# A short convolution's first products: ten of them in front, units loaded twice, squares summed by DMAs

## The chip, the cores and the metric

The kernel runs on one core of a Trainium2 chip. The metric is the device time of one execution in microseconds (us); the time of a version is the median of its runs. TensorE (PE) multiplies matrices, VectorE (DVE) and ScalarE (ACT) work element by element, GpSimd (POOL) and SyncE (SP) here only start DMAs. Each engine executes its own instructions in order, and semaphores tie the engines together.

## The reference

A decoder trunk of two layers on a sequence of 1024 positions with 1024 features, in float32. Layer 0 mixes by a short gated convolution, layer 1 by dilated attention; each is followed by a SwiGLU block. The change is in layer 0's mixer, and there in its first projection:

```python
def rms_norm(x, g):
    xf = x.astype(jnp.float32)
    y = xf * lax.rsqrt(jnp.mean(xf * xf, axis=-1, keepdims=True) + EPS)
    return (y * g.astype(jnp.float32)).astype(x.dtype)

def short_conv_mixer(h, w_in, conv_k, w_out):
    b, c, u = jnp.split(h @ w_in, 3, axis=-1)
    y = lax.conv_general_dilated(c * u, conv_k[:, None, :], window_strides=(1,),
        padding=[(CONV_WIDTH - 1, 0)], dimension_numbers=("NWC", "WIO", "NWC"),
        feature_group_count=D_MODEL)
    return (b * y) @ w_out

h = rms_norm(x, mix_norm[0])
x = x + short_conv_mixer(h, conv_w_in[0], conv_kernel[0], conv_w_out[0])
```

## The kernel before

A float32 product is made of three matmuls in a reduced format: every operand is split into a high part (a copy by ACT, L137, L497 or L803) and a low part (the difference, by DVE, L138, L498 or L804), and L505 to L507 multiply high by high, high by low and low by high.

The projection `h @ w_in` goes by Winograd's form of Strassen's method. The weights are cut into twelve units u of two tiles each (a "raw" tile is 128 x 1024 floats, 512 KB). A unit has seven products m, each of four times three matmuls of 128x128 by 128x512, and so of twelve. Products 1, 2 and 4 take a quarter of the unit's weights as it is; 6, 7, 5 and 3 take sums of quarters, which `add_pair` makes on DVE (L185, "combo") ahead of the split. The other side, operand m, is a quarter of X times the norm's gain or a sum of such quarters; `operands` makes the seven of them once, in the order 1, 2, 6, 7, 5, 4, 3, and all units share them. The scale of the norm (the mean of squares) is applied later, to the products' results, so products can start before it is known.

The results of a unit gather in two or three of the eight banks of PSUM ("p", "q", "r"); `save` copies a bank out (L511, ACT), `add` adds a bank to such a copy (L515, DVE). `first(u)` is the add for products 1 and 2 of a unit, and frees the bank q.

The order of products is written by hand in `unit_order`: before, (0,1), (1,1), (0,2), (1,2), (2,1), (2,2), (3,1), then the sixth and seventh products of units 0 and 1 and so on, a pair (u, m) being product m of unit u. `mix` says beside which product which other work is recorded: `start(n)` runs after the n-th product, `next(prep)` goes one step on in `operands`, `ensure(at(u, m))` makes weights up to (u, m). What is recorded first stands first in each engine's queue. `squares` squares tiles of X on ACT (L394, L398) and adds them into the tile `acc` on DVE (L400); `stats` then sums over partitions by eight small matmuls (L417), and a second step spreads the result (L433).

Weights come by DMAs from SP. `load_first` issues the first ones in a fixed order, halves of X between them; `load_raw(upto)` issues later ones (L151), up to a number that each unit's table `ahead` gives for a product. Tiles live in a ring of 41 pages: a page that is freed is taken again, and who takes it waits for its last reader.

Of the kernel before, what the change touches and what calls it, by code (L numbers as in the profile page):

```python
# [23 lines left out]
HALF = 512  # L24
# [70 lines left out]
def trunk(ctx: ExitStack, tc: tile.TileContext, x, gains_in, cwi, ck, cwo, wqkv, wo, relb,  # L95
# [19 lines left out]
    def half(h):  # L115
        return slice(h * HALF, (h + 1) * HALF)
# [61 lines left out]
    def add_pair(u, rows, w, eng, upto, low=()):  # L178


        t = {}

        def combo(a, b, op):
            c = half_page("combo")[:, :w]
            eng.tensor_tensor(out=c, in0=a, in1=b, op=op)  # L185
# [65 lines left out]
    def unit_order(nu, conv):  # L251

        order = [(0, 1), (1, 1), (0, 2), (1, 2), (2, 1), (2, 2), (3, 1)]
        if conv:
            order += [(0, 6), (1, 6), (3, 2)] + [(u, m) for m in (7, 5, 4, 3) for u in (0, 1)]
            order += [(2, 6), (2, 5), (2, 7)]
        else:
            order += [(3, 2)] + [(u, m) for m in (6, 7, 4, 5, 3) for u in (0, 1)] + [(2, 6), (2, 5), (2, 7)]
        order += [(3, 6), (2, 4), (2, 3), (3, 5), (3, 7), (4, 1)] + [(4, 2)] * conv + [(3, 4), (3, 3)]
# [11 lines left out]
    def add_units(key, nu, column):  # L271
# [1 line left out]
        units, slabs, base = [], {}, len(raw_src)  # L273
        raw_base[key] = base
        for u in range(nu):
            rows = ((0, 1), (2, 5), (3, 6), (4, 7))[u] if u < 4 else (2 * u, 2 * u + 1)
            for n in range(2):
                slabs[rows[n]] = column(u, n)
            if u < 4 or key == CONV:
                a = ((2, 5), (3, 7), (4, 7), (4, 9))[u] if u < 4 else (2 * u + 3, 2 * u + 3)  # L280
                ahead = {m: a[m > 2] for m in WINOGRAD}
                if key != CONV and u < 2:
# [12 lines left out]
        raw_src.extend(slabs[r] for r in range(2 * nu))  # L295
        ops.extend(units[u][m] for u, m in unit_order(nu, key == CONV))

    def add_down(key, w, pairs, chunk, last):
# [174 lines left out]
    class Strassen:  # L473
# [73 lines left out]
        def whole(self, u, m, d):  # L547
# [16 lines left out]
            if m == 2 and u > 3 or (u, m) == (0, 4):  # L564
                for x in (u,) if u else range(4):
                    self.out(x, (0, 0), self.first(x))
                    del self.st[x]["u1"]

# [222 lines left out]
    class Conv(Strassen):  # L791
# [12 lines left out]
            nc.vector.scalar_tensor_tensor(lo, t, self.norm.gain(n), hi, op0=ALU.mult, op1=ALU.subtract)  # L804

        def squares(self, ns, h):
            for n in ns:
                self.norm.square(n, h * HALF, h * HALF + HALF, eng=nc.vector)

        def operands(self):  # L810
            gain, stt = self.norm.gain, nc.vector.scalar_tensor_tensor
# [7 lines left out]
            t3, t2 = [half_page("t3") for k in range(4)], [half_page("t2") for k in range(4)]  # L819
            for k in range(4):  # L820
                nc.scalar.activation(t3[k], X[k][:, b], AF.Identity, scale=gain(k))
            for m in (6, 7, 3):
                combos[CONV, 0](m)
            lo = None
            for k in range(4):
                stt(t3[k], X[4 + k][:, b], gain(4 + k), t3[k], op0=ALU.mult, op1=ALU.subtract)
# [16 lines left out]
            yield  # L843
            for k in range(4):
                self.operand(5, k, k, X[k][:, b])
            for k in range(4):
                stt(t2[k], X[4 + k][:, a], gain(4 + k), t2[k], op0=ALU.mult, op1=ALU.subtract)
            yield
# [3 lines left out]
            yield  # L852
            for k in range(4):
                self.operand(3, k, 4 + k, X[4 + k][:, b])
            X[:4] = [None] * 4

        def pad(self, t, h):

# [101 lines left out]
        def mix(self, group1):  # L960
            norm = self.norm
            prep = self.operands()
            stats = norm.stats(0, S)
            late = [(k, h) for h in range(2) for k in range(4, KT)]

            def start(n):
                if n == 0:
# [2 lines left out]
                elif n == 1:  # L970
                    next(prep)
                elif n == 2:
                    ensure(self.at(3, 1))
                    next(prep)
                elif n == 3:
                    ensure(self.at(0, 6))
                    combos[CONV, 1](6)
                    combos[CONV, 1](7)
                    next(prep)
                    ensure(self.at(1, 6))  # L980
                    self.squares(range(4), 1)
                elif n == 4:
                    ensure(self.at(0, 7))
                    next(prep)
                elif n == 7:
                    ensure(self.at(1, 7))
                    next(prep)
                    ensure(self.at(1, 5))
                elif n == 8:
                    next(prep)  # L990
                    ensure(self.at(1, 4))
                elif n == 11:
                    self.first(1)
                    next(prep, None)
                    ensure(self.at(1, 3))
                elif n == 18:
                    self.ahead = 3
                for _ in range({7: 1, 9: 2, 11: 2, 12: 3}.get(n, 0)):
                    k, h = late.pop(0)
                    self.squares((k,), h)  # L1000
                    if h:
                        X[k] = None

            def gather():
                for u in range(1, 4):
                    if "q" in self.st[u]:
                        self.first(u)
                next(stats)

            def spread():  # L1010
# [788 lines left out]
```

## Time and profile before

| | |
|---|---|
| median of 3 runs | 2215.94 us (2215.3 to 2217.3) |
| the profiled execution | 2215.37 us, of which the profile's span is 2213.6 |
| mean granted PE clock | 0.985 |
| DMA from 4 to 24 us | 300 to 414 GB/s |
| DMA from 26 to 35 us | none |
| last product of this stage, (11,3) | starts at 260.19 us |

A row of the timeline gives the start, the duration, the engine, the line, the operation, out<-in and the shapes; the bracket is the idle time of the engine before it and what ended it. "PE" rows are matmuls, "PEld" the loads of their weights. The matmuls of one product start 0.23 us apart at full clock though each is shown as 0.39 long, because they are pipelined.

### The profile page before, as it was taken

Reading aid. Unit: us, or ns where it says so; the run is one execution under the profiler, and the core shown is the slowest. Engines: PE = TensorE matmul, PEld = TensorE weight load, DVE = VectorE, ACT = ScalarE, POOL = GpSimd, SP = SyncE. Lnnn points to the kernel's source line nnn. Section 1 sums busy time; section 2 is a strip of 40 time slices with the busy share of each in tenths; the row PEclk is TensorE's granted clock in tenths of the full one; section 3 lists DMA queues with packets and bytes.
Section 4 is the critical chain, followed back from the end, with each engine's and each line's share of the span. In section 5 each row is a group of like instructions: output and inputs, shape, how many; then the busy total and the mean of one; then the engine's idle time right before and its main releaser. Section 6 shows DMA issues by size and latency. Waiting matters only on the chain.

```text
span 2213.6 us, 30526 instructions
## 1 busy us (share of the span) xinstructions
PE 2143.2 (97%) x11138; PEld 1829.8 (83%) x11138; DVE 1769.8 (80%) x3255; ACT 998.4 (45%) x1808; POOL 147.9 (7%) x196
## 2 busy tenths in 40 slices
PE   7899999899999999999999999999899999999998
PEld 5788887688888878878999999887678888878887
DVE  7797758888888798965677767868988888889886
ACT  6433425444444444434455555534534444444435
POOL 0000000010101000010111111110010101000000
PEclk9999999999999999999999999999999999999999
DMA  4122541222323374423333333544113323266432
GB/s 154 53 84 74 208 131 51 86 98 90 117 93 114 106 269 153 131 86 131 90 90 91 90 90 83 168 130 140 62 72 102 113 96 119 96 218 210 155 93 77
DMA packets 131263, 255.30 MB, mean 115 GB/s; under 512 B 47386, under 2 KB 58666, under 8 KB 131114
## 3 DMA queue, kind: packets, MB, share of 16 engines
q1 hardware_dynamic: 75978, 184.80, 26.2%
q0 software_dynamic: 13968, 45.46, 5.6%
q10 hardware_dynamic: 41168, 23.10, 3.6%
q8 instruction: 88, 1.44, 0.3%
q14 instruction: 61, 0.50, 0.1%
HBM read 187.04 MB, written 66.26 MB: 114 GB/s over the span
## 4 chain that ended last, share of the span: by engine, by line
PE 79%; DVE 11%; ACT 4%; DMA 3%; issue 2%; ACTq 0%; SPq 0%; DVEq 0%
PE bank L505 16%; PE bank L507 16%; PE bank L506 16%; PE bank L346 5%; PE bank L348 5%; PE bank L347 5%; PE bank L1425 4%; PE bank L600 2%; PE bank L599 2%; PE bank L597 2%; DVE b L498 2%; DVE w L138 2%; PE bank L1353 1%; PE bank L1352 1%; DVE x L438 1%
## 5 line engine op out<-in xcount | busy, mean ns | idle before, releaser
L505 PE MATMUL bank<-b,w 128*128 128x512 f32 x1784 | 706.1, 396 | 27.2 <-DVE part L515 7.3
L507 PE MATMUL bank<-b,w 128*128 128x512 f32 x1784 | 702.7, 394 | 15.8 <-DVE w L138 15.8
L506 PE MATMUL bank<-b,w 128*128 128x512 f32 x1784 | 702.7, 394 | 2.1 <-DVE b L498 2.1
L505 PEld LDWEIGHTS bank<-b,w 128*128 128x128 f32 x1784 | 339.8, 190 | 102.4 <-ACT w L137 10.5
L507 PEld LDWEIGHTS bank<-b,w 128*128 128x128 f32 x1784 | 339.4, 190 | 91.9 <-DVE w L138 20.3
L506 PEld LDWEIGHTS bank<-b,w 128*128 128x128 f32 x1784 | 340.0, 191 | 73.3 <-DVE b L498 2.9
L137 ACT ACTIVATE w<-combo 128x512 fp32r<-128x512 f32 (+2 forms) x464 | 235.0, 535 | 279.2 <-DVE combo L185 273.4
L138 DVE TENSOR_TENSOR w<-combo,w 128x512 fp32r<-128x512 f32 (+2 forms) x464 | 260.6, 575 | 69.2 <-ACT w L137 67.2
L511 ACT ACTIVATE part<-bank 128x512 f32<-128x512 f32 x168 | 99.2, 594 | 276.1 <-PE bank L507 273.6
L138 DVE TENSOR_TENSOR w<-raw,w 128x512 fp32r<-128x512 f32 (+2 forms) x316 | 168.9, 559 | 20.8 <-ACT w L137 19.1
L515 DVE TENSOR_TENSOR part<-part,bank 128x256 f32<-128x256 f32 (+1 forms) x348 | 158.6, 486 | 31.0 <-PE bank L507 15.5
L137 ACT ACTIVATE w<-raw 128x512 fp32r<-128x512 f32 (+2 forms) x316 | 150.2, 520 | 45.7 <-PE bank L507 11.3
L726 DVE TENSOR_TENSOR x<-x,bank 128x512 f32<-128x512 f32 x168 | 114.2, 680 | 30.9 <-PE bank L507 30.9
L346 PE MATMUL bank<-w_hi,w 128*128 128x512 f32 (+1 forms) x320 | 122.0, 381 | 0.0
L348 PE MATMUL bank<-w_hi,w 128*128 128x512 f32 (+1 forms) x320 | 120.0, 375 | 0.7 <-DVE w L138 0.7
L347 PE MATMUL bank<-w_lo,w 128*128 128x512 f32 (+1 forms) x320 | 119.8, 374 | 0.0
L438 DVE TENSOR_TENSOR x<-x,bank 128x512 f32<-128x512 f32 (+1 forms) x104 | 65.9, 641 | 62.6 <-PE bank L348 53.8
L185 DVE TENSOR_TENSOR combo<-raw 128x512 f32<-128x512 f32 (+1 forms) x160 | 102.9, 643 | 4.3 <-DMA raw<-in_conv_w_in 4.3
L346 PE MATMUL bank<-h_hi,w_hi 128*128 128x512 f32 x256 | 104.6, 409 | 0.7 <-ACT w_hi L137 0.7
L348 PE MATMUL bank<-h_hi,w_lo 128*128 128x512 f32 x256 | 100.2, 391 | 0.7 <-DVE w_lo L138 0.7
L347 PE MATMUL bank<-h_lo,w_hi 128*128 128x512 f32 x256 | 99.9, 390 | 0.0
L1111 ACT ACTIVATE part<-part 128x512 f32<-128x512 f32 x66 | 39.7, 628 | 110.6 <-DVE part L515 110.6
(237 smaller groups left out, 3835.2 us busy)
## 6 DMA issues: line engine op xcount, KB each, us to landing
hin<-part SPq DMA_DIRECT2D x126, 256.0 KB
raw<-in_ffn_w_gate SPq DMA_DIRECT2D x44, 512.0 KB
raw<-in_ffn_w_up SPq DMA_DIRECT2D x44, 512.0 KB
part<-sum POOLq DMA_DIRECT2D x72, 256.0 KB, 3.0
raw<-in_ffn_w_down SPq DMA_DIRECT2D x48, 384.0 KB
x<-spill SPq DMA_DIRECT2D x24, 512.0 KB
raw<-in_attn_w_qkv SPq DMA_DIRECT2D x24, 512.0 KB
raw<-in_conv_w_in SPq DMA_DIRECT2D x21, 512.0 KB
```

Source lines behind the costliest of these rows:

```text
L137: nc.scalar.activation(hi, src, AF.Copy)
L138: eng.tensor_tensor(out=lo, in0=src, in1=hi, op=ALU.subtract)
L185: eng.tensor_tensor(out=c, in0=a, in1=b, op=op)
L346: nc.tensor.matmul(b, whi[:, a], ahi[:, s], start=first, stop=False)
L347: nc.tensor.matmul(b, whi[:, a], alo[:, s], start=False, stop=False)
L348: nc.tensor.matmul(b, wlo[:, a], ahi[:, s], start=False, stop=last)
L505: nc.tensor.matmul(b, hi[:, a], bhi, start=start and k == 0, stop=False, skip_group_check=True)
L506: nc.tensor.matmul(b, hi[:, a], blo, start=False, stop=False, skip_group_check=True)
L507: nc.tensor.matmul(b, lo[:, a], bhi, start=False, stop=k == n - 1, skip_group_check=True)
L511: nc.scalar.activation(t, b, AF.Copy)
L515: nc.vector.tensor_tensor(out=t, in0=t, in1=b, op=ALU.add)
L726: nc.vector.tensor_tensor(out=X[n][:, half(h)], in0=X[n][:, half(h)], in1=b, op=ALU.add)
```

## The change

- **The order of products.** Ten products that need only operands 1 and 2 now stand in front, two of each of units 0 to 4: (3,2), (4,1) and (4,2) come ahead of (0,6). Then come 6, 7, 5 and 4 of units 0 and 1 in turn, (2,6), (2,7), (0,3), (1,3), (2,5), and from (3,6) on the order is as it was, without (4,1) and (4,2). The statistics' two steps hang on (0,3) and (2,5) where they hung on (2,6) and (2,7).
- **Raw tiles.** The table of rows gives the place of each unit's tiles in the order of loads. Units 2, 3 and 4 now have their first tile early, for products 1 and 2, and load it a second time beside their second tile, for the products with m > 2, so that its page is free in between: three loads more. `load_first` issues seven raw tiles where it issued five (tiles 4, 1, 5, 6).
- **Squares.** ACT still squares; the sums into `acc` are now fourteen accumulating DMAs of 256 KB, issued by POOL from page `sq`, for k = 1 to 7 in two halves.
- **Hooks.** `start`, `gather` and `operands` are written anew to go with it: no weight combination stands ahead of operand 6, `first(0)` to `first(4)` are called at fixed places, and all of X is given up after operand 3.

```diff
         def raw(m, n, h):
             load_raw(upto(m))
-            return raw_tile[rows[n]][:, h * w:h * w + w]
+            return raw_tile[rows[2 if n == 0 and m > 2 and len(rows) > 2 else n]][:, h * w:h * w + w]
...
         if conv:
-            order += [(0, 6), (1, 6), (3, 2)] + [(u, m) for m in (7, 5, 4, 3) for u in (0, 1)]
-            order += [(2, 6), (2, 5), (2, 7)]
+            order += [(3, 2), (4, 1), (4, 2)] + [(u, m) for m in (6, 7, 5, 4) for u in (0, 1)]
+            order += [(2, 6), (2, 7), (0, 3), (1, 3), (2, 5)]
...
+            if key == CONV:
+                rows = ((0, 1), (2, 6), (3, 7, 8), (4, 9, 10), (5, 11, 12))[u] if u < 5 else (2 * u + 3, 2 * u + 4)
...
+            for n in range(len(rows)):
+                slabs[rows[n]] = column(u, n % 2)
+            if key == CONV:
+                a = {0: (6, 6, 6, 7, 7), 1: (6, 6, 7, 8, 8), 2: (8, 9, 9, 10, 10), 3: (10, 11, 12, 12, 13),
+                     4: (12, 14, 13, 14, 15)}.get(u, (2 * u + 6,) * 5)
+                ahead = dict(zip((6, 7, 5, 4, 3), a))
+                ahead.update({m: 6 if u < 5 else 2 * u + 6 for m in (1, 2)})
...
         def squares(self, ns, h):
+            norm = self.norm
+            if norm.acc is None:
+                norm.acc, norm.rstd = page("acc"), page("rstd")
             for n in ns:
-                self.norm.square(n, h * HALF, h * HALF + HALF, eng=nc.vector)
+                if n == 0:
+                    nc.scalar.activation(norm.acc[:, half(h)], X[n][:, half(h)], AF.Square)
+                else:
+                    sq = page("sq")[:, :HALF]
+                    nc.scalar.activation(sq, X[n][:, half(h)], AF.Square)
+                    nc.gpsimd.dma_start(out=norm.acc[:, half(h)], in_=sq, accum_op=ALU.add)
...
-            for m in (6, 7, 3):
-                combos[CONV, 0](m)
...
                 elif n == 2:
-                    ensure(self.at(3, 1))
+                    ensure(self.at(4, 1))
+                    self.squares(range(4, KT), 0)
                     next(prep)
                 elif n == 3:
-                    ensure(self.at(0, 6))
-                    combos[CONV, 1](6)
-                    combos[CONV, 1](7)
+                    ensure(self.at(4, 2))
+                    self.first(0)
                     next(prep)
-                    ensure(self.at(1, 6))
                     self.squares(range(4), 1)
                 elif n == 4:
+                    self.first(1)
+                    ensure(self.at(1, 6))
+                elif n == 5:
                     ensure(self.at(0, 7))
+                    self.squares(range(4, KT), 1)
...
-            self.run(start, {(2, 6): gather, (2, 7): spread})
+            self.run(start, {(0, 3): gather, (2, 5): spread})
...
-        for i in range(5):
+        for i in range(7):
             raw_tile[i] = page("raw")
-        raw_state[0] = 5
+        raw_state[0] = 7
...
-        nc.sync.dma_start(raw_tile[4], raw_src[4])
-        nc.sync.dma_start(raw_tile[1], raw_src[1])
+        for i in (4, 1, 5, 6):
+            nc.sync.dma_start(raw_tile[i], raw_src[i])
```

DVE's queue behind the splits for the first six products, before. The combos are those of unit 0's weights, L826 and L827 make operand 6, L498 and L138 are second halves of operands and weights.

```order
L138 TENSOR_TENSOR w<-raw,w 128x512 x3
L185 TENSOR_TENSOR combo<-raw 128x512
L185 TENSOR_TENSOR combo<-combo,raw 128x512
L185 TENSOR_TENSOR combo<-raw 128x512
L185 TENSOR_TENSOR combo<-raw,combo 128x512
L826 SCALAR_TENSOR_TENSOR t_316<-x,gains,t_316 128x512
L827 SCALAR_TENSOR_TENSOR t_320<-x,gains,t_316 128x512
L826 SCALAR_TENSOR_TENSOR t_317<-x,gains,t_317 128x512
L827 SCALAR_TENSOR_TENSOR t_321<-x,gains,t_317 128x512
L498 TENSOR_TENSOR b<-t_320,b 128x512
L138 TENSOR_TENSOR w<-raw,w 128x512
```

The same place in the changed kernel, from the third tile of operand 6 on (L842 to L843 make operand 6, L507 and L138 are second halves, L524 is `add`). Before these rows stand the first half of operand 6 and the three splits for (3,1), (3,2) and (4,1).

```order
L138 TENSOR_TENSOR w<-raw,w 128x512 x3
L842 SCALAR_TENSOR_TENSOR t_323<-x,gains,t_323 128x512
L843 SCALAR_TENSOR_TENSOR t_327<-x,gains,t_323 128x512
L507 TENSOR_TENSOR b<-t_326,b 128x512
L842 SCALAR_TENSOR_TENSOR t_324<-x,gains,t_324 128x512
L843 SCALAR_TENSOR_TENSOR t_328<-x,gains,t_324 128x512
L507 TENSOR_TENSOR b<-t_327,b 128x512
L507 TENSOR_TENSOR b<-t_328,b 128x512
L185 TENSOR_TENSOR combo<-raw 128x512
L185 TENSOR_TENSOR combo<-combo,raw 128x512
L138 TENSOR_TENSOR w<-raw,w 128x512
L524 TENSOR_TENSOR part<-part,bank 128x512
```

Operand 6 moved ahead of the combinations, and `first(0)`, the last row, stands behind them and behind the split of tile 5 (the third of the first row).

POOL's queue now, up to its first stores of the convolution's output:

```order
L1649 DMA taps<-in_conv_kernel 128x24
L1650 DMA eye<-in_identity 128x128
L826 DMA acc<-sq 128x512 x14
L673 DMA plain_conv_162<-y 128x512
L673 DMA plain_conv_163<-y 128x512 x2
```

The row of fourteen is new. ACT's queue now, around operands 5 and 3; the brackets name the semaphores that a row waits for, and those that begin with DMASW belong to POOL's DMAs:

```order
L812 ACTIVATE b<-x,gains 128x512 [waits DMASW1_49,DVE_49,Activation_49]
L812 ACTIVATE b<-x,gains 128x512 [waits DVE_49]
L812 ACTIVATE b<-x,gains 128x512 [waits DMASW2_49,DVE_49,Activation_49]
L812 ACTIVATE b<-x,gains 128x512 [waits DVE_49,Activation_49]
L137 ACTIVATE w<-combo 128x512 [waits DMASW3_49]
L520 ACTIVATE part<-bank 128x512 [waits PE_49]
L137 ACTIVATE w<-combo 128x512 [waits Activation_49]
```

```order
L137 ACTIVATE w<-raw 128x512 [waits DMAHW2_49]
L812 ACTIVATE b<-x,gains 128x512 [waits DMASW6_49]
L812 ACTIVATE b<-x,gains 128x512 [waits PE_49,Activation_49]
L812 ACTIVATE b<-x,gains 128x512 [waits DMASW7_49]
L812 ACTIVATE b<-x,gains 128x512 [waits DVE_49,PE_49]
```

These rows take pages that squares held: the eighth, ninth, tenth, thirteenth and last accumulation must have landed before them. The last two of those rows are the third and fourth tile of operand 3.

More of the change, by code (lines that the diff above doesn't have):

```diff
@@ L275, in add_units @@
         for u in range(nu):
[L276 to L280, printed above, removed]
+            if key == CONV:
+                rows = ((0, 1), (2, 6), (3, 7, 8), (4, 9, 10), (5, 11, 12))[u] if u < 5 else (2 * u + 3, 2 * u + 4)
+            else:
+                rows = ((0, 1), (2, 5), (3, 6), (4, 7))[u] if u < 4 else (2 * u, 2 * u + 1)
+            for n in range(len(rows)):
[5 more added lines that the diff above has]
+                ahead.update({m: 6 if u < 5 else 2 * u + 6 for m in (1, 2)})
+            elif u < 4:
+                a = ((2, 5), (3, 7), (4, 7), (4, 9))[u]
                 ahead = {m: a[m > 2] for m in WINOGRAD}
-                if key != CONV and u < 2:
+                if u < 2:
                     ahead = ({1: 2, 2: 3, 6: 4, 7: 5, 4: 5, 5: 5, 3: 5}, {1: 3, 2: 4, 6: 5, 7: 5, 4: 6, 5: 6, 3: 7})[u]
@@ L294, in add_units @@
                          lambda i, u=u: base + 2 * u + {1: 1, 2: 1, 3: 3, 4: 3}.get(i, 2))
-        raw_src.extend(slabs[r] for r in range(2 * nu))
+        raw_src.extend(slabs[r] for r in range(len(slabs)))
         ops.extend(units[u][m] for u, m in unit_order(nu, key == CONV))
@@ L563, in whole @@
                 self.out(u, (1, 1), self.add(d.pop("u3"), d["r"]))
-            if m == 2 and u > 3 or (u, m) == (0, 4):
-                for x in (u,) if u else range(4):
+            if m == 2 and u > 4 or (u, m) == (0, 4) or self.key == CONV and (u, m) == (3, 7):
+                for x in {0: range(4), 3: (4,)}.get(u, (u,)):
                     self.out(x, (0, 0), self.first(x))
@@ L972, in start @@
                 elif n == 2:
[L973 removed]
+                    ensure(self.at(4, 1))
+                    self.squares(range(4, KT), 0)
                     next(prep)
                 elif n == 3:
[L976 to L978 removed]
+                    ensure(self.at(4, 2))
+                    self.first(0)
                     next(prep)
[L980 removed]
                     self.squares(range(4), 1)
                 elif n == 4:
+                    self.first(1)
+                    ensure(self.at(1, 6))
+                elif n == 5:
                     ensure(self.at(0, 7))
[L984 to L988, printed above, removed]
+                    self.squares(range(4, KT), 1)
                 elif n == 8:
                     next(prep)
[L991 removed]
+                elif n == 10:
+                    self.first(2)
                 elif n == 11:
[L993 removed]
+                    next(prep)
+                    self.first(3)
+                elif n == 12:
+                    next(prep)
+                elif n == 13:
+                    next(prep)
+                    self.first(4)
+                elif n == 15:
                     next(prep, None)
[L995 to L996 removed]
+                elif n == 20:
                     self.ahead = 3
[L998 to L1002, printed above, removed]
             def gather():
[L1005 to L1007 removed]
                 next(stats)
```

7 lines of the change are left out of this document (4 added, 3 removed).

## The prediction

> **What bounds the kernel now.** The page comes first. TensorE (PE) is busy for 97% of the span, so a change can only win where PE waits or runs at a lower clock.
>
> ```profile
> span 2213.6 us, 30526 instructions
> PE 2143.2 (97%) x11138; PEld 1829.8 (83%) x11138; DVE 1769.8 (80%) x3255; ACT 998.4 (45%) x1808; POOL 147.9 (7%) x196
> ```
>
> The windows tell where. The columns are PE, PEld, DVE, ACT and POOL busy, the granted PE clock, the DMA share and GB/s. From 200 to 220 us PE is busy throughout at clock 1.00; in the first 100 us it is busy for 81, with stretches at half clock.
>
> ```profile
> 20.00:22.00 2.00, 2.00 (x11) 1.65 (x10) 0.00 (x0) 0.00 (x0) 0.00 (x0) 1.00 1.04 414
> 24.00:26.00 2.00, 1.22 (x6) 0.68 (x4) 1.97 (x4) 0.00 (x0) 0.00 (x0) 1.00 0.30 121
> 30.00:35.00 5.00, 5.00 (x13) 3.33 (x11) 4.84 (x8) 2.45 (x5) 0.00 (x0) 0.54 0.00 0
> 60.00:65.00 5.00, 5.00 (x13) 3.89 (x13) 1.60 (x3) 0.48 (x1) 0.00 (x0) 0.50 0.00 0
> 70.00:75.00 5.00, 2.87 (x13) 2.09 (x12) 4.56 (x9) 3.86 (x7) 0.00 (x0) 1.00 0.08 14
> 0.00:100.00 100.00, 81.02 (x314) 61.95 (x315) 75.44 (x124) 56.37 (x95) 1.44 (x6) 0.93 0.30 106
> 200.00:220.00 20.00, 20.00 (x90) 16.53 (x89) 15.13 (x29) 6.85 (x13) 1.62 (x3) 1.00 0.29 93
> ```
>
> PE's timeline gives the waits one by one (in brackets the idle time before a row, and what ended it).
>
> ```profile
> 11.09 0.40 PE L505 MATMUL bank<-b,w 128*128 128x512 f32 x1
> 16.89 0.39 PE L505 MATMUL bank<-b,w 128*128 128x512 f32 x1
> 18.03 0.39 PE L507 MATMUL bank<-b,w 128*128 128x512 f32 x1
> 20.75 0.39 PE L507 MATMUL bank<-b,w 128*128 128x512 f32 x1
> 22.34 0.39 PE L505 MATMUL bank<-b,w 128*128 128x512 f32 x1
> 28.98 0.79 PE L505 MATMUL bank<-b,w 128*128 128x512 f32 x1 [3.76 <-ACT w L137]
> 36.52 0.50 PE L507 MATMUL bank<-b,w 128*128 128x512 f32 x1 [1.33 <-DVE w L138]
> 59.67 0.80 PE L505 MATMUL bank<-b,w 128*128 128x512 f32 x1 [4.25 <-DVE part L515]
> 72.89 0.47 PE L505 MATMUL bank<-b,w 128*128 128x512 f32 x1 [2.13 <-DVE part L515]
> ```
>
> 18.03 and 20.75 are twelve matmuls apart, so a product (u, m), which is twelve matmuls, takes 2.72 us when nothing is missing. (2,2), the sixth product, starts at 22.34 and (0,3), the seventeenth, at 72.89: eleven products in 50.55 us where 11 x 2.72 = 29.9 would do. **20.6 us** are lost there: waits, and the half clock (0.54 and 0.50 in the windows) after the waits of 3.76 and 4.25; after the one of 2.13 the clock stays at 1.00. Who is late is VectorE (DVE):
>
> ```profile
> 16.07 1.89 DVE L138 TENSOR_TENSOR w<-raw,w 128x512 fp32r<-128x512 f32 x3
> 22.22 0.69 DVE L185 TENSOR_TENSOR combo<-raw 128x512 f32<-128x512 f32 x1 [4.26 <-DMA raw<-in_conv_w_in]
> 24.76 0.74 DVE L826 SCALAR_TENSOR_TENSOR t<-x,gains,t 128x512 f32<-128x512 f32 x1
> 43.21 2.49 DVE L842 TENSOR_TENSOR x<-x 128x512 f32<-128x512 f32 x4
> 45.61 0.68 DVE L515 TENSOR_TENSOR part<-part,bank 128x512 f32<-128x512 f32 x1
> 46.81 2.73 DVE L804 SCALAR_TENSOR_TENSOR b<-x,gains,b 128x512 fp32r<-128x512 f32 x4
> 49.47 2.73 DVE L847 SCALAR_TENSOR_TENSOR t<-x,gains,t 128x512 f32<-128x512 f32 x4
> 10.62 1.66 ACT L398 ACTIVATE sq<-x 128x512 f32<-128x512 f32 x3
> 17.16 2.56 ACT L821 ACTIVATE t<-x,gains 128x512 f32<-128x512 f32 x4
> ```
>
> DVE stands 4.26 us at the weight combination of unit 0, whose raw tile 1 lands at 22.2, with the work for operand 6 queued behind it; then it works without a pause while PE waits. Four tensor_tensors start 2.40 us apart from what follows (0.60 each), four scalar_tensor_tensors 2.66 (0.67 each). Among its work until 75 us are the sums of squares (the first row), and part of it waits for ACT (the second; behind the second bar the idle time before, and what ended it):
>
> ```profile
> L400 DVE TENSOR_TENSOR acc<-acc,sq 128x512 f32<-128x512 f32 x13 | 8.9, 688 | 1.1 <-ACT sq L398 0.6
> L804 DVE SCALAR_TENSOR_TENSOR b<-x,gains,b 128x512 fp32r<-128x512 f32 x16 | 11.2, 747 | 6.7 <-ACT b L803 6.6
> ```
>
> There are fourteen such sums by the code, k = 1 to 7 in two halves.
>
> **The change, part by part.**
>
> *Ten products in front.* They use operands 1 and 2 alone, and each costs DVE one split (0.60) against 2.72 on PE. DVE is free at 16.07 + 1.89 = 18.0, the upper halves of X are there (ACT's L821 starts at 17.16 without a wait), so operand 6 begins 6.8 us earlier than now (24.76). What is late next is (4,1). Units 0 to 3 fill the eight banks, so the ninth needs the bank that the add of first(0) releases, and on DVE that add stands behind raw tile 5. The tile comes one load behind tile 1: 0.52 MB at 408 to 414 GB/s, so 22.2 + 1.3 = 23.5, and up to 1.3 later for the first accumulations in the same full DMA stretch; I take 24.3. Then 1.2 for the split on ACT and DVE, 4 x 0.67 + 3 x 0.60 for the rest of operand 6, 3 x 0.60 for two combinations and the split of (4,2), 0.7 for the add: 32.5. PE would be there at 16.89 + 5 x 2.72 = 30.5. A wait of 2.0, up to 3 if the loads are later; I take **2.4**, nearer the idle time of 2.13, which kept the clock, than 3.76, which lost it. Up to (0,6), at 30.5 + 2.4 + 2 x 2.72 = 38.3, DVE has eight tensor_tensors, 4.8, and ends at 37.3: no wait.
>
> *From (0,6) to (2,6)* PE has 8 x 2.72 = 21.8 us. DVE has, by its order, 26 tensor_tensors and 12 scalar_tensor_tensors before the second half of the weight of (2,6) is there: 15.6 + 8.0 = 23.6. It ends at 37.3 + 23.6 = 60.9, and the third matmul of (2,6), which is the first to use that half, could start at 38.3 + 21.8 + 0.45 = 60.5. So DVE still sets the pace, by 0.4 us at the least; with handovers from ACT, which cost DVE 6.7 us at sixteen instructions of L804, up to 5. I take **3.5**, and **1.0** for a second bank wait and the small ones after (2,6). The column sums of the statistics and their spreading only change places: nothing.
>
> *Squares by DMA.* DVE loses 14 x 0.60 = 8.4 us, already left out of the 23.6. In their place stands a chain: thirteen of the fourteen accumulations wait for the one before, since they add to the same tile, and each frees the page that a later ACT instruction takes. POOL has nothing else to do then. One link is the wake of POOL after its releaser and the time to landing. No accumulating transfer is in this trace; the nearest rows are plain stores:
>
> ```profile
> plain_conv<-y POOLq DMA_DIRECT2D x16, 256.0 KB, 2.5
> odram<-o POOLq DMA_DIRECT2D x7, 512.0 KB, 2.9
> DMA to landing us min/median/max: 2.3/2.5/5.1
> 102.90 0.68 DVE L899 TENSOR_TENSOR y<-y,part 128x512 f32<-128x512 f32 x1
> 103.88 0.54 POOL L664 DMA_DIRECT2D plain_conv<-y  x1 [101.37 <-DVE y L899]
> ```
>
> The wake is 103.88 - 103.58 = 0.3. Landing: 2.3 for the fastest store of 256 KB, 5.1 for the slowest (the third row is L664's), and 2.9 for 512 KB, which is what an accumulation of 256 KB must read. So T is 2.6 to 5.4, and I take **3.2**. The first three run under the full loads and with the slowest landing end at 11.2 + 3 x 5.4 = 27.4, where 11.2 is the end of the first square (10.62 + 0.6); the fourth square, behind ACT's split of tile 5, exists by 25.5. From 27, ten further links in series and 0.56 for one that starts beside another end at 27.6 + 10T: 59.6. The last one is waited for by ACT for the third tile of operand 3, which ACT must have 3.3 us (0.7 on ACT, two scalar_tensor_tensors, two tensor_tensors) before DVE ends that half of the weight of (2,6): 60.5 + 3.5 - 3.3 = 60.7, about 60 with ACT's own queue. T = 3.24 is the edge: below it nothing is gained, and above it each 0.1 us costs 1.0, since ACT is in order and the copies out of the banks queue behind that wait. Being that near, I add **1.0**.
>
> The Trainium skill says that an accumulation reads two sources for one write ("Collectives: The Full Stack", The bandwidth ceiling), and gives a GpSimd DMA 2.0 us + bytes / 436 GB/s ("DMA: Bandwidth & Descriptors", Anatomy of one DMA — SWDGE (gpsimd) path). For 256 KB that is 2.6 against 2.5 in the row; with two reads 3.2, an estimate from these pages, and by it T would be 3.5, the chain would end at 62.6 and the time would be about 2206. It speaks against the change, as it makes what DVE did in 0.6 us a step of 3.
>
> *Raw tiles loaded twice:* three loads of 512 KB, 1.3 us each at the rate above, at a time when DMA is 8 to 30% busy; hidden, and if not, 1.3 to 4 us.
>
> *Sum:* 20.6 - 2.4 - 3.5 - 1.0 - 1.0 = **12.7 us** less. Everything after (2,5) keeps its order and moves up. The profiled run took 2215.37, 0.57 under the median of 2215.94: 2215.9 - 12.7 = **2203**.
>
> **Rivals.**
> - *The front starves on loads* (0.10). For it: DMA is full (1.04) until 24 us, and accumulations now share it. Against: fewer weight loads stand behind tile 5 than now. If tile 5 is 3 us late, the wait at (4,1) is 5.4, PE falls to half clock (some 13 matmuls of 0.43 for 0.23, 2.6 us): 12.7 - 5.6 = 7 less, 2209.
> - *The chain eats the gain* (0.15). T of 3.8 to 4.6: the added wait is 6 to 14 us, in pieces, one or two of them over 3 us with a half clock behind. 2209 to 2219, no change to tell at the upper part.
> - *Slower: the chain sets the pace* (0.17). One mechanism: from T = 4.2 (half clocks counted) to 4.6 (not) the last accumulation comes later than all that was saved. With 5.4 the chain ends at 81.6, 21.6 us after its edge: 2215.9 - 13.7 + 21.6 = 2224, to 2229 with two half clocks. For it: the slowest store took just that. Against: it stood among other traffic, the median was 2.5.
> - *It doesn't do what it says:* excluded; the order shows the products, the pages' waits and no L400 left in this stage.
>
> **How the numbers follow.** Forecast 0.58 (2200 to 2208). Loads 0.10, chain 0.15, slower 0.17. A measurement of this kernel tells 0.2% (4.4 us) from no change: below 2211.5 is faster, above 2220.4 slower. The forecast, the loads and a fifth of the chain case are faster: 0.71; the rest of the chain case and a little of the slow one are the same: 0.13; slower 0.16. The range is 2199 (T of 2.6 and 1.0 for the pace of DVE) to 2224 (T of 5.4 without half clocks).
>
> **What would show it.** PE: no wait of 3.76 before (3,1), ten products from 5.5 us on with one wait of 2 to 3 before (4,1), started by the add of a part and a bank; the clock at 1.00 from 11 to 70 us. POOL: fourteen accumulations with starts about 3.2 apart from the fourth on, the last landing near 60. (0,3) would start near 70 rather than 72.89 though four more products stand ahead of it. ACT's rows of b waiting for an accumulating DMA, and starts more than 4 us apart on POOL, would prove the forecast wrong.

## The result, and the profile after

The changed kernel takes 2216.89 us (median of 14 runs, 2213.5 to 2219.7) against 2215.99 before: a ratio of 1.0003, with a 95% interval of 0.9996 to 1.0010. There is no difference to be told. The profiled execution took 2213.53, of which the span is 2211.7; it is the fastest of the fourteen.

In the two traces the stage ends almost together: (11,3), its last product, starts at 260.19 before and at 258.99 now. 20.6 us were lost between (2,2) and (0,3) before. Now (2,2) starts at 22.21 and (0,3) at 82.05, with fifteen products in 59.84 us where 15 x 2.72 = 40.8 would do, so 19.0 are lost; the prediction left 7.9.

PE's timeline of the changed kernel, the rows that waited (start, length, line, shapes, and in the bracket the idle time and what ended it), and those with which (4,2), (0,6) and (0,3) start:

```profile
34.67 0.77 PE L514 MATMUL bank<-b,w 128*128 128x512 f32 x1 [4.14 <-DVE part L524]
39.93 0.44 PE L514 MATMUL bank<-b,w 128*128 128x512 f32 x1
42.73 0.39 PE L514 MATMUL bank<-b,w 128*128 128x512 f32 x1
55.16 0.50 PE L514 MATMUL bank<-b,w 128*128 128x512 f32 x1 [1.39 <-ACT w L137]
63.40 0.50 PE L514 MATMUL bank<-b,w 128*128 128x512 f32 x1 [1.70 <-ACT w L137]
73.07 0.50 PE L514 MATMUL bank<-b,w 128*128 128x512 f32 x1 [3.67 <-ACT w L137]
82.05 0.39 PE L514 MATMUL bank<-b,w 128*128 128x512 f32 x1
```

The windows of the same kernel (PE, PEld, DVE, ACT and POOL busy, granted PE clock, DMA share, GB/s):

```profile
34.00:42.00 8.00, 7.33 (x21) 5.86 (x22) 7.97 (x14) 5.43 (x11) 2.03 (x3) 0.62 0.39 68
60.00:65.00 5.00, 3.30 (x14) 2.11 (x13) 4.34 (x8) 2.31 (x5) 1.08 (x2) 1.00 0.39 68
70.00:75.00 5.00, 1.14 (x3) 0.71 (x4) 3.08 (x5) 2.48 (x4) 0.00 (x0) 0.91 0.47 126
0.00:100.00 100.00, 81.29 (x324) 62.60 (x325) 66.74 (x107) 55.42 (x94) 13.40 (x20) 0.95 0.54 154
```

(4,1) waits 4.14 and then runs at half clock: it takes 39.93 - 34.67 = 5.26 instead of 2.72. From (0,6) at 42.73 to (0,3) there are ten products, 27.2, in 39.3 us. DVE did get rid of its sums: over the first 100 us it is busy for 66.74 instead of 75.44. Behind (0,6) PE's long waits name ACT, not DVE. Who is late now stands in ACT's and POOL's timelines:

```profile
25.75 0.63 ACT L137 ACTIVATE w<-raw 128x512 fp32r<-128x512 f32 x1 [2.61 <-DMA raw<-in_conv_w_in]
54.47 0.63 ACT L137 ACTIVATE w<-combo 128x512 fp32r<-128x512 f32 x1 [2.73 <-DMA acc<-sq]
58.96 2.20 ACT L506 ACTIVATE b<-t 128x512 fp32r<-128x512 f32 x4 [2.36 <-DMA acc<-sq]
62.71 1.15 ACT L137 ACTIVATE w<-raw 128x512 fp32r<-128x512 f32 x2 [1.55 <-DMA acc<-sq]
67.25 1.34 ACT L812 ACTIVATE b<-x,gains 128x512 fp32r<-128x512 f32 x2 [3.39 <-DMA acc<-sq]
71.16 1.33 ACT L812 ACTIVATE b<-x,gains 128x512 fp32r<-128x512 f32 x2 [2.57 <-DMA acc<-sq]
```

```profile
11.42 0.92 POOL L826 DMA_DIRECT2D acc<-sq  x1 [8.89 <-ACT sq L825]
18.64 0.87 POOL L826 DMA_DIRECT2D acc<-sq  x1 [6.31 <-ACT t L839]
26.43 0.85 POOL L826 DMA_DIRECT2D acc<-sq  x1 [6.92 <-ACT w L137]
30.19 0.84 POOL L826 DMA_DIRECT2D acc<-sq  x1 [2.91 <-DMA acc<-sq]
34.00 0.85 POOL L826 DMA_DIRECT2D acc<-sq  x1 [2.98 <-ACT b L506]
37.83 0.84 POOL L826 DMA_DIRECT2D acc<-sq  x1 [2.97 <-DMA acc<-sq]
41.66 1.71 POOL L826 DMA_DIRECT2D acc<-sq  x2 [2.99 <-ACT sq L825]
...
59.39 0.84 POOL L826 DMA_DIRECT2D acc<-sq  x1 [3.56 <-DMA acc<-sq]
63.22 0.85 POOL L826 DMA_DIRECT2D acc<-sq  x1 [2.99 <-DMA acc<-sq]
67.76 0.84 POOL L826 DMA_DIRECT2D acc<-sq  x1 [3.69 <-DMA acc<-sq]
```

The first of ACT's rows is the split of raw tile 5, which waits for its load. The other five wait for accumulations, for the pages that squares hold, and PE's waits at 55, 63 and 73 us (behind (1,7), (1,5) and (1,4)) are for weights (L137) that stand behind them in ACT's queue. POOL starts an accumulation 3.8 us after the one before in quiet stretches and up to 4.5 after it (63.22 to 67.76) beside weight loads; the last starts at 67.76, and ACT's row at 71.16 waits for it. Where a bracket of POOL's names ACT, the square had been made before (the first three by 12.15): POOL waits there for the accumulation before it to land.

Two theories were tried. **A, the chain:** the serial accumulations set the pace from (0,6) on. **B, the front:** raw tile 5 comes late, at 25.75, because the first accumulations share the loads' DMA time, so the bank for (4,1) is late. A rival of both, **C**, was that DVE is still the bound.

### The profile page after: what moved, and what is told of

Same layout as the page of the kernel before. It is cut to its first block, busy times and chain, and to the rows that moved or that the text cites. A ratio compares the mean times of both kernels' runs of the same rounds, so it can differ in the third digit from the quotient of the medians.

```text
span 2211.7 us, 30560 instructions
## 1 busy us (share of the span) xinstructions
PE 2142.0 (97%) x11138; PEld 1829.3 (83%) x11138; DVE 1761.6 (80%) x3241; ACT 998.2 (45%) x1808; POOL 159.6 (7%) x210
## 4 chain that ended last, share of the span: by engine, by line
PE 79%; DVE 10%; ACT 4%; DMA 4%; issue 2%; ACTq 0%; SPq 0%; DVEq 0%; POOLq 0%
PE bank L514 16%; PE bank L516 16%; PE bank L515 16%; PE bank L357 5%; PE bank L355 5%; PE bank L356 5%; PE bank L1438 4%; PE bank L608 2%; PE bank L609 2%; PE bank L606 2%; DVE b L507 2%; DVE w L138 1%; PE bank L1366 1%; PE bank L1365 1%; DMA acc<-sq 1%
## 5 line engine op out<-in xcount | busy, mean ns | idle before, releaser
L137 ACT ACTIVATE w<-combo 128x512 fp32r<-128x512 f32 (+2 forms) x464 | 235.1, 535 | 290.4 <-DVE combo L185 280.7
L138 DVE TENSOR_TENSOR w<-combo,w 128x512 fp32r<-128x512 f32 (+2 forms) x464 | 261.3, 576 | 77.2 <-ACT w L137 74.4
L138 DVE TENSOR_TENSOR w<-raw,w 128x512 fp32r<-128x512 f32 (+2 forms) x316 | 169.3, 561 | 24.7 <-ACT w L137 23.0
L524 DVE TENSOR_TENSOR part<-part,bank 128x256 f32<-128x256 f32 (+1 forms) x348 | 159.3, 488 | 29.2 <-PE bank L516 17.1
L137 ACT ACTIVATE w<-raw 128x512 fp32r<-128x512 f32 (+2 forms) x316 | 150.3, 520 | 49.9 <-PE bank L516 11.3
```

What stands on the lines that cost most here:

```text
L137: nc.scalar.activation(hi, src, AF.Copy)
L138: eng.tensor_tensor(out=lo, in0=src, in1=hi, op=ALU.subtract)
L524: nc.vector.tensor_tensor(out=t, in0=t, in1=b, op=ALU.add)
```

## The experiments

All ratios are to the kernel before, run on the same chip as the experiment (e1 to e4, e5 to e8, e9 and e10 each ran on one chip, where the kernel before took 2215.9, 2215.4 and 2216.3). The last three columns are from the traces: where (0,6), (0,3) and the stage's last product start. A trace is one execution: what follows the stage's last product took from 1952.6 to 1957.4 us in the profiled executions of these twelve kernels, so differences of one or two us at the stage's end say nothing of the median. The change ends the stage 1.2 us earlier in its trace, its fastest execution, and is no faster.

| | median us | ratio [95%] | (0,6) | (0,3) | (11,3) |
|---|---|---|---|---|---|
| before | 2215.99 | | | | 260.19 |
| the change | 2216.89 | 1.0003 [0.9996, 1.0010] | 42.73 | 82.05 | 258.99 |
| e1 first adds early | 2220.29 | 1.0018 [1.0009, 1.0026] | 36.65 | 86.56 | 263.50 |
| e2 two chains | 2208.81 | 0.9966 [0.9954, 0.9979] | 42.93 | 73.86 | 254.56 |
| e3 both | 2207.59 | 0.9958 [0.9944, 0.9971] | 37.25 | 69.72 | 252.02 |
| e4 as e1, no sums | 2199.59 | 0.9927 [0.9915, 0.9940] | 35.96 | 66.89 | 243.82 |
| e5 as e3, join by DMA | 2203.37 | 0.9949 [0.9935, 0.9962] | 36.77 | 69.31 | 246.25 |
| e6 as e5, late squares | 2202.91 | 0.9947 [0.9935, 0.9960] | 35.57 | 68.54 | 245.48 |
| e7 plain copies | 2203.88 | 0.9949 [0.9936, 0.9961] | 40.70 | 72.31 | 249.24 |
| e8 as e1, sums on DVE | 2209.34 | 0.9971 [0.9961, 0.9982] | 37.49 | 74.28 | 253.54 |
| e9 the change, no sums | 2200.59 | 0.9928 [0.9915, 0.9940] | 37.83 | 68.67 | 245.60 |
| e10 as e6, squares earlier | 2200.65 | 0.9932 [0.9918, 0.9946] | 36.09 | 69.47 | 246.41 |

From (0,6) to (0,3) there are ten products in all the new versions, 27.2 us; what it takes beyond that is lost. It is 12.1 in the change, 22.7 in e1, 3.7 with two chains (e2), 4.4 with copies (e7) and 3.6 without sums (e9).

**e1: the adds that free the banks, early.**

```diff
                 elif n == 2:
+                    self.first(0)
                     ensure(self.at(4, 1))
...
                 elif n == 3:
+                    self.first(1)
                     ensure(self.at(4, 2))
-                    self.first(0)
...
                 elif n == 4:
-                    self.first(1)
                     ensure(self.at(1, 6))
```

> first(0) and first(1) are called one product earlier, ahead of the split of tile 5, so the bank for (4,1) is free when PE comes. Theory A (the chain of fourteen accumulations sets the time through ACT's waits for pages): the wait of 4.14 before (4,1) goes and comes back at ACT's next wait for an accumulation, the chain still ends near 71, 2214 to 2217. Theory B (the front sets the time: tile 5 late, bank late, half clock behind): 4.1 + 2.5 are gained and kept, about 2210. Theory C (DVE has too much work, whoever waits): no change, 2216 to 2217.

The front's loss went as B says: (4,1) follows without a wait, and (0,6) starts 6.1 us earlier. And yet the kernel is 0.2% slower than before the change, above what any of the three theories gave it. POOL's timeline shows the last two accumulations, and ACT's the row that waits for the first of them to land:

```profile
62.96 0.85 POOL L826 DMA_DIRECT2D acc<-sq  x1 [2.98 <-DMA acc<-sq]
71.06 0.84 POOL L826 DMA_DIRECT2D acc<-sq  x1 [7.25 <-DMA acc<-sq]
```

```profile
70.56 1.33 ACT L812 ACTIVATE b<-x,gains 128x512 fp32r<-128x512 f32 x2 [8.62 <-DMA acc<-sq]
```

The chain did not move forward with PE, as A says. It even ended later than in the change, since its last link but one took 8.1 us, from 62.96 to 71.06. Beside it run weight loads that SP issued from 62.45 on; a row of SP's queue and one of the windows show them. The row merges three issues: two by 63.43, and a third only at 70.22. The DMA share is 0.71 between 66 and 74 us:

```profile
62.45 8.10 SPq L151 DMA_DIRECT2D raw<-in_conv_w_in  x3
```

```profile
66.00:74.00 8.00, 2.74 (x11) 1.80 (x10) 3.31 (x5) 1.33 (x2) 0.84 (x1) 0.89 0.71 182
```

Time that is won ahead of a chain which binds is only waited for behind it, and here two loads ran beside one of its links; that they made it long was not tested by itself.

**e2: two chains, joined by one addition on DVE. e3: both.**

```diff
+                self.accs = [norm.acc, page("acc_odd")]
             for n in ns:
-                if n == 0:
-                    nc.scalar.activation(norm.acc[:, half(h)], X[n][:, half(h)], AF.Square)
+                acc = self.accs[n % 2]
+                if n < 2:
+                    nc.scalar.activation(acc[:, half(h)], X[n][:, half(h)], AF.Square)
...
-                    nc.gpsimd.dma_start(out=norm.acc[:, half(h)], in_=sq, accum_op=ALU.add)
+                    nc.gpsimd.dma_start(out=acc[:, half(h)], in_=sq, accum_op=ALU.add)
...
             def gather():
+                odd = self.accs.pop()
+                nc.vector.tensor_tensor(out=norm.acc, in0=norm.acc, in1=odd, op=ALU.add)
```

> Even and odd tiles are summed into two accumulators, twelve accumulations in two chains side by side, and one DVE add of 128 x 1024 joins them. A: from the fourth on a pair takes the 3.8 that one link takes now, the last one lands near 50 rather than 71, ACT's waits for accumulations go, and 5 to 8 us are gained: 2209 to 2212. B: nothing is gained, as (4,1) still waits 4.1 at its bank: 2216. C: 2216, or 1 more for the add.

> The edits of e1_first_early and e2_two_chains together. A alone: as e2_two_chains, 2209 to 2212. A and B: both kinds of wait go, 9 to 13 us less, 2204 to 2208. C: 2216 to 2217.

With two chains the time falls by 8.1 us, as A says (0.2 more than its band). The waits on ACT behind (1,7), (1,5) and (1,4) are gone and the last accumulation starts at 46.9. From (0,6) to (0,3) only 3.7 us are lost instead of 12.1, about as much as without any sums. The front is as late as in the change; PE's wait at (4,1) in e2:

```profile
34.65 0.76 PE L514 MATMUL bank<-b,w 128*128 128x512 f32 x1 [4.30 <-DVE part L524]
```

With both edits the front is mended too: (0,6) starts 5.7 us earlier than in e2. Of that 2.5 reach the stage's end, and the times of e2 and e3 lie 1.2 apart with overlapping intervals, so a gain from B is not shown here. What is left of a price is the join, which DVE comes to after other work; PE's timeline of e3 shows the column sums waiting for it:

```profile
74.52 3.07 PE L426 MATMUL bank<-ones,acc 128*128 128x1 f32 x16 [1.92 <-DVE acc L1024]
```

**e4: as e1, with the accumulations left out.**

```diff
-                    nc.gpsimd.dma_start(out=norm.acc[:, half(h)], in_=sq, accum_op=ALU.add)
```

> first(0) and first(1) early, and the fourteen accumulations left out: the squares of tiles 1 to 7 are made and not added, so the norm's scale is that of tile 0 alone. It shows what the order of products gives without any cost of the sums. A and B: 13 to 16 us less, 2200 to 2203, and no wait of ACT for a page. C: at most 3 less, 2213 or more.

The same order and the same DVE work as e1, without the chain: 20.7 us less, 0.4 below the band expected. C falls with it, since no wait of PE on DVE over 1.3 us is left in the stage. Beside e3 it also shows what two accumulations do to the loads. DVE's splits that use raw tile 5, first in e3, then in e4, whose first products start alike at 5.45 us:

```profile
26.64 0.69 DVE L138 TENSOR_TENSOR w<-raw,w 128x512 fp32r<-128x512 f32 x1 [1.25 <-ACT w L137]
```

```profile
23.88 0.69 DVE L138 TENSOR_TENSOR w<-raw,w 128x512 fp32r<-128x512 f32 x1 [0.81 <-ACT w L137]
```

Tile 5 is 2.76 us later with two accumulations of 256 KB ahead of it, 1.4 for each: about what a load of 512 KB took there (1.3 by the rate in the prediction).

**e5: the join as one more accumulating DMA. e6: the first two accumulations put off until tile 5 is in.**

```diff
                     self.squares(range(4, KT), 1)
+                    odd = self.accs.pop()
+                    nc.gpsimd.dma_start(out=norm.acc, in_=odd, accum_op=ALU.add)
...
-                odd = self.accs.pop()
-                nc.vector.tensor_tensor(out=norm.acc, in0=norm.acc, in1=odd, op=ALU.add)
```

```diff
-            self.squares(range(4), 0)
+            self.squares(range(2), 0)
...
+                    self.squares(range(2, 4), 0)
                     self.squares(range(4), 1)
```

> As e3 (two chains, first(0) and first(1) early), but the odd accumulator is added into the other by one more accumulating DMA of 512 KB right behind the last squares, in place of VectorE's join before the statistics. In e3 the last accumulation started at 46.6, so the join should start near 50.5 and land by 56, well before (0,3) near 68. If e3's wait of 1.9 and long (0,3) (7.73 for 4.4) were due to the late VectorE join, about 3 us come back: 2204 to 2205, with (0,3) again about 4.4 long. If it is the column sums themselves that are late, the time stays at 2207.6.

> As e5, but the first two accumulations (beside the full loads at 11 to 18 us) are put off until tile 5 is in; the first squares go straight into the two accumulators. Theory that an accumulation beside the loads takes its bytes from them (two accumulations, 2.5 us of tile 5 between e3 and e4): tile 5's split at 23.2 instead of 26.0, no wait at (4,1) or (4,2), 2 to 3 us less than e5: 2201 to 2203, near the 2199.6 of e4 that has no sums. Rival, that tile 5 was late for another reason: split at 26, same time as e5. If the chain of twelve then ends too late, waits on an accumulating DMA come back in ACT's rows.

e5 came as expected, 0.6 better than the band: (0,3) is 4.42 long again. Its interval overlaps that of e3, though its slowest run (2204.35) is below the fastest of e3 (2205.38). In e6 the front went as expected (ACT's split of tile 5 starts at 22.80 against 25.52 in e5, ten products run without a pause, (0,6) at 35.57), but only 0.8 us of it reached the stage's end, and the times of e5 and e6 can't be told apart. ACT's timeline of e6 shows where it went:

```profile
52.24 1.15 ACT L506 ACTIVATE b<-t 128x512 fp32r<-128x512 f32 x2 [2.52 <-DMA acc_odd<-sq]
53.30 1.13 ACT L137 ACTIVATE w<-raw 128x512 fp32r<-128x512 f32 x2
57.37 2.57 ACT L812 ACTIVATE b<-x,gains 128x512 fp32r<-128x512 f32 x4 [2.94 <-DMA acc<-acc_odd]
```

PE then waits 1.54 for the weight at 53.30, and the join is the next link that ACT waits for.

**e7: the chain kept, with copies in place of accumulations.**

```diff
-                    nc.gpsimd.dma_start(out=norm.acc[:, half(h)], in_=sq, accum_op=ALU.add)
+                    nc.gpsimd.dma_start(out=norm.acc[:, half(h)], in_=sq)
```

> The change as it is, but its thirteen serial transfers copy instead of accumulating (the sum of squares is left out: the scale is then that of the last square alone), so each moves the same bytes out with one read instead of two and still waits for the one before. If the second read and the accumulate make the link of 3.8 long, a copy's link is about 3.0 (issue 0.54, landing 2.5), the last starts near 60 instead of 68, the waits on ACT at (1,7), (1,5), (1,4) shrink to under 3 together, and the time is 2204 to 2208. If a link is mostly the fixed cost of a GpSimd DMA and its wake, it stays at 3.5 or more and the time at 2213 to 2217.

This measures a link of copies against one of accumulations. POOL's timeline of e7 in the quiet stretch, then the last line of the view of the tile `acc`, in e7 and in the change:

```profile
27.29 0.55 POOL L826 DMA_DIRECT2D acc<-sq  x1 [2.60 <-ACT sq L825]
30.13 0.55 POOL L826 DMA_DIRECT2D acc<-sq  x1 [2.29 <-DMA acc<-sq]
32.97 0.55 POOL L826 DMA_DIRECT2D acc<-sq  x1 [2.29 <-ACT b L506]
...
56.29 0.55 POOL L826 DMA_DIRECT2D acc<-sq  x1 [5.38 <-DMA acc<-sq]
59.11 0.55 POOL L826 DMA_DIRECT2D acc<-sq  x1 [2.28 <-DMA acc<-sq]
```

```profile
DMA to landing us min/median/max: 2.2/2.3/6.0
```

```profile
DMA to landing us min/median/max: 3.2/3.3/7.3
```

A copy's link is 2.84 us, an accumulation's 3.82; one link of e7, the one before 56.29, took 5.9 (50.37 to 56.29). All of the difference is in the landing (2.3 and 3.3); what lies between a landing and the next start is 0.5 in both. With the link at 2.84 the last start comes at 59.1 instead of 67.8, one wait of 0.9 on ACT's weights is left, and the time falls by 13, to the lower edge of what was expected. Not all of that is the chain's: in the traces 7.7 us less are lost behind (0,6) and 2.2 less before it, where the copies hold up tile 5 less (ACT's split of it starts at 24.88). The wait at (4,1) is still there, shorter, as PE's timeline and the window around it show:

```profile
33.81 0.77 PE L514 MATMUL bank<-b,w 128*128 128x512 f32 x1 [3.15 <-DVE part L524]
```

```profile
33.00:38.00 5.00, 4.19 (x13) 3.40 (x14) 4.96 (x10) 3.09 (x7) 1.60 (x3) 0.66 0.32 121
```

**e8: the same order as e1, with the sums on DVE as before the change.**

```diff
             for n in ns:
-                if n == 0:
...
+                self.norm.square(n, h * HALF, h * HALF + HALF, eng=nc.vector)
```

> The new order with first(0) and first(1) early, but the fourteen sums of squares on VectorE as before the change, 0.60 us each (8.4 in all), in the places where the changed kernel starts its DMAs. No chain through a DMA is left. If VectorE sets the pace after (0,6), as the prediction had it, the 8.4 come back as waits of 4 to 8 us more than in e4: 2204 to 2208, most of it near (4,1), (4,2) and (0,6), and it is near e3's 2207.6. If VectorE had slack, 2200 to 2202. Against 2220.3 for the same order with one chain of DMAs, either would say that this one chain is worse than the sums that it replaced.

1.3 us above the upper end expected; against e4 the stage ends 9.7 us later, of which 14 x 0.60 = 8.4 are the sums themselves. PE's longest wait on DVE is 3.18, in (0,6), behind three of them. With the change's order of products and the adds early, the old way of summing is 11 us faster than the one chain (e1) and 6 slower than two chains joined by DMA (e5).

**e9: the change as it is, without the accumulations** (the edit of e4 alone).

> The change in its own order (first(0) behind the rest of operand 6, as changed), with the accumulations alone left out (the scale is that of the first tile's square). It parts the two causes: the chain through the accumulating DMAs and the late bank at (4,1). If both hold as the runs so far show, tile 5's split comes at 23.2 instead of 25.7, the wait at (4,1) is 1.5 to 2.0 instead of 4.1 and keeps the clock, none of the waits on ACT at (1,7), (1,5), (1,4) are left, and the time is 2.0 above e4's 2199.6: 2201 to 2202.5, some 15 below the change. If the bank wait did not depend on the accumulations, it stays near 4 with the half clock behind it, and the time is 2205 to 2206.

It tells whether the bank wait, too, comes from the accumulations. PE's wait at (4,1):

```profile
32.02 0.47 PE L514 MATMUL bank<-b,w 128*128 128x512 f32 x1 [1.73 <-DVE part L524]
```

```profile
32.00:36.00 4.00, 3.94 (x16) 3.02 (x17) 3.96 (x7) 2.31 (x5) 0.00 (x0) 1.00 0.00 0
```

ACT's split of tile 5 starts at 23.09 instead of 25.75, the wait is 1.73, and the window's clock stays at 1.00: the accumulations cause most of the bank wait as well as the chain. The time of 2200.59 is 16.3 below the change and 0.4 below the expected band. It was to be 2.0 above e4's; it is 1.0 above, with overlapping intervals, so what the early adds are worth without sums is not shown.

**e10: as e6, with the last four squares one hook earlier.**

```diff
                 elif n == 4:
                     ensure(self.at(1, 6))
+                    self.squares(range(4, KT), 1)
...
                 elif n == 5:
                     ensure(self.at(0, 7))
-                    self.squares(range(4, KT), 1)
```

(The join moves with the squares.)

> As e6, with the last four squares of the second half put one hook earlier (beside the fifth product instead of the sixth), so that the last accumulations start near 37 to 43 instead of 39.6 to 45.0, ahead of the three weight loads that SP issues at 44.1. In e6 the last accumulation took 7.2 us beside these loads, ACT waited 2.5 for it (operand 4) and 2.9 for the join, and PE lost 1.9 at (1,5) and 2.5 at half clock in (0,4). If the collision with the loads is the cause, these waits fall below 1 and the time is 2200 to 2201.5, within 2 of e4, which has no sums. If the three links at the end are too long in any case, the waits only shrink by what the start moved, and the time stays at 2202 to 2203.

The time fell into the expected band by luck, since the starts and waits that were to bring it there did not come. POOL's timeline of e10:

```profile
40.95 0.85 POOL L828 DMA_DIRECT2D acc<-sq  x1 [2.94 <-ACT w L137]
...
46.30 0.84 POOL L828 DMA_DIRECT2D acc_odd<-sq  x1 [0.65 <-ACT part L520]
53.56 0.85 POOL L1005 DMA_DIRECT2D acc<-acc_odd  x1 [6.41 <-DMA acc_odd<-sq]
```

The last accumulation starts at 46.30, later than in e6 (44.99), and ACT still waits 4.10 and 2.94 for the DMAs. (Of the three loads named for e6, two were issued at 44.06 and the third at 55.43, behind the last accumulation.) In the traces the stage even ends 0.9 later than in e6. The intervals of e5, e6 and e10 overlap: these three beat both kernels by 0.5 to 0.7%, and which of them is best was not settled. Whether the last link can be kept clear of the weight loads wasn't tried further; by the stage's end in e4, which has no sums, 1.7 to 2.6 us are left in it.

## Why the prediction was wrong

It forecast 2203, 12.7 us less; nothing was gained. The time lies in its range of 2199 to 2224, at the upper part of the rival called "The chain eats the gain", which had a chance of 0.15. That the rival's time fits so well is in part luck: it meant the chain alone, and 4.5 of what was lost beyond the sum came at the bank for (4,1). The bookkeeping against the traces, in us lost beyond 2.72 a product:

| | predicted | the change | e9, no sums |
|---|---|---|---|
| (2,2) to (0,6), the bank for (4,1) | 2.4 | 6.9 | 2.3 |
| (0,6) to (0,3), DVE's pace and small waits | 4.5 | | 3.6 |
| (0,6) to (0,3), the chain | 1.0 | | 0 |
| (0,6) to (0,3) together | 5.5 | 12.1 | 3.6 |
| sum | 7.9 | 19.0 | 5.9 |

- **The step that failed is the size of T, "I take 3.2".** It measured 3.8 in quiet stretches (0.5 from landing to the next start, where 0.3 was taken, and 3.3 to land, where 2.9 was) and up to 4.5 beside loads; from the fourth start to the last landing the links took 4.0 each on average. The first three links, which were to end near 27, ended just before the fourth started at 30.19: the first two took 7.2 and 7.8 under the full loads, where the slowest store of 5.1 had been the bound. So the last landing came near 71 instead of 59.6, of which 3.2 is the later start and the rest the longer links, and 8.5 us (12.1 - 3.6) were paid where 1.0 stood. The nearest row, a plain store of twice the size, stood for a transfer that reads two tiles; that was the wrong neighbour by 0.4, at a place where each 0.1 cost 1.0 by the prediction's own words.
- The Trainium skill's estimate in the prediction (landing 3.2 from "DMA: Bandwidth & Descriptors", Anatomy of one DMA — SWDGE (gpsimd) path, with two reads) was nearer: the trace has 3.3. For a copy the same formula gives 2.6, and e7 has 2.3, so an accumulation costs 1.0 more than a copy, not 0.6.
- **The edge held as far as it was tried.** The prediction set the limit at T = 3.24. With T = 2.84 (e7) the chain cost 0.8 (4.4 against 3.6 in e9), with 3.82 it cost 8.5; nothing between was run. That e7 took 2203.9, near the 2203 forecast, is partly luck: 4.8 were lost before (0,6) instead of 2.4, and the chain landed at 61.4 where 27.6 + 10 x 2.84 gives 56.0.
- **The bank wait was mis-sized too.** The sum to 2.4 allowed "up to 1.3 later for the first accumulations" and took tile 5 at 24.3; ACT's split waited for it until 25.75. Each accumulation ahead of it held up the loads by about as much as a load of 512 KB takes (e3 and e4). The wait became 4.14 and lost the clock, another 2.54. Without accumulations it is 1.73 (e9), and the loss from (2,2) to (0,6) is 2.3, near the 2.4 predicted. Mended alone (e1) it gained nothing, because the chain took it back.
- **DVE's pace was nearly right:** 3.5 and 1.0 for small waits stood there, 3.6 came for both (e9). So was the claim that the sums cost DVE 8.4: with them back on DVE the stage ends 9.7 later (e8 against e4).
- Without chain the sum would have read 12.7 + 1.0 = 13.7 and 2202; e9 took 2200.6. The order of products does what it was counted for: (3,1) follows (2,2) without a wait at 24.93, where it stood at 28.98 behind a wait of 3.76. That the raw tiles loaded twice cost nothing fits with this sum, but was not tested by itself.
- The rival in which the chain is slower still (from T = 4.2) did not come in the change, but something like it did in e1: with one link of 8.1 us the last accumulation started 3.3 later than in the change, and the kernel was 0.2% slower than before.
- Both signs that the prediction named as proof against it stand in the trace: ACT's rows of b that wait for an accumulating DMA (58.96, 67.25 and 71.16), and starts more than 4 us apart on POOL (63.22 to 67.76).

## What to carry to other kernels

Here work that moved from a busy engine to DMAs turned its 0.6 us a step into a latency of 3.8; where such steps depend on one another, count links times the whole time from start to start, ask who takes the pages that the links hold, and break the chain (two accumulators took 8.1 us off the changed kernel) before anything else is tuned. A gain ahead of such a chain was worth nothing while the chain bound (e1); with the chain cut, 2.5 of 5.7 us reached the stage's end in the traces, and the times can't be told apart (e2 and e3). Where a forecast sits on an edge, an unmeasured duration (T, here) deserves the chance of its whole range, not a point with a small allowance.

## What the runs showed of the hardware

- An accumulating DMA of 256 KB from SBUF to SBUF, issued by GpSimd, occupies POOL for 0.85 us and lands after 3.3 (median, the change); the same copy without accumulation 0.55 and 2.3 (e7). From a landing to the next start 0.5 us pass in both where the next one waits for it.
- Beside full loads the first two accumulations of the change took 7.2 and 7.8 us from start to start; two of them delayed raw tile 5 by 2.8, 1.4 each (e3 against e4).
- How much clock an idle time cost at (4,1): after 1.73 the clock stayed at 1.00 (e9, the product 3.00 long), after 3.15 the product took 4.17 (e7), after 4.14 it took 5.26 (the change). These are single executions, and a product without a wait takes 2.72.
